# Weight matrices stored as contiguous blocks, and GpSimd's work around the routing softmax put behind it

## The chip, the cores and the metric

One core of one Trainium2 chip runs the whole program. The metric is the device time of one execution in microseconds (us). The median of 3 runs before is 2841.9 us, from 2841.22 to 2849.14. A profile of a further execution shows when each instruction ran on the five engines (PE, the matrix engine; DVE, VectorE; ACT, ScalarE; POOL, GpSimd; SP, which here only issues transfers) and what each transfer moved.

## The reference, cut to what matters

Two blocks run one after the other on 1024 tokens of 1024 features (float32).

The first block modulates a normalised input by vectors made from `silu(c) @ w_ada + b_ada`, multiplies it with `w_in` (1024 x 4624), runs a bidirectional recurrent memory (mLSTM) and a Fourier branch, merges the branches with `w_fourier` and `w_mlstm`, multiplies with `w_out`, and adds the result to `x`. It ends in a layer of 16 experts, each of which takes its 128 best tokens:

```python
def expert_choice(h, w_router, w_gate, w_up, w_down):
    b, l, _ = h.shape
    cap = CAP_FACTOR * l // N_EXPERTS
    aff = jax.nn.softmax(jnp.einsum('bld,de->ble', h, w_router).astype(jnp.float32), axis=-1)
    vals, idx = lax.top_k(jnp.swapaxes(aff, 1, 2), cap)
    bidx = jnp.arange(b)[:, None, None]
    xs = h[bidx, idx]
    hid = jax.nn.silu(jnp.einsum('becd,edf->becf', xs, w_gate)) * jnp.einsum('becd,edf->becf', xs, w_up)
    y = jnp.einsum('becf,efd->becd', hid, w_down) * vals[..., None].astype(h.dtype)
    return jnp.zeros_like(h).at[bidx, idx].add(y)
```

The second block has two layers of gated attention. Each computes `z = rms_norm(x) @ w_in`, cuts z into queries, keys, values and gates of several heads, attends, and returns `x + mixed @ w_out`. The even layer's `w_in` is 1024 x 4104, so a row of it is 16,416 bytes long; the odd layer's is 1024 x 3328, with rows of 13,312 bytes.

## The kernel before

**Products.** Every float32 product of a weight and an activation is made as three matmuls (`mm3`, lines 190 to 194) from a rounded high part and a low part of both operands. `split` (line 196) makes the parts: ACT or POOL copies the high part, and DVE or POOL subtracts it from the raw value for the low part.

**Weights.** Outside the experts, weights come in chunks of 256 columns. `Chunk.dma(j)` (line 1414) loads 128 columns of all 1024 rows into the tile `lwr` (128 partitions x 8 x 128, 512 KB), where row k*128+p of the matrix goes to partition p. The matrices lie in memory as the reference has them, row after row, so that such a load is 1024 pieces of 512 bytes, one row pitch apart. `Chunk.split(j)` makes `lwh` and `lwl` from it, on ACT and DVE. There are two `lwr` buffers. `w_ada` is loaded in blocks of 256 columns (tiles `wt` in `start`, line 327, and `awt` in `ada_late`, line 940), in pieces of 1024 bytes. A chunk of the merge takes three loads, from `w_fourier`, `w_fourier_r` and `w_mlstm` (line 223). The experts' weights (`ewr`, lines 977 to 991) are loaded in whole rows, pieces of 4096 bytes, through a ring of 13 buffers of 1 MB.

**Queues.** All these loads are issued by SP, in program order, and SP waits at a load until its buffer is free. ACT issues the small moves `qh<-qh` and `kY<-klo` of 128 KB, which carry the low or high part of queries and keys to the other half of the partitions (lines 1532 and 1548). POOL issues the experts' gathers and scatters.

**Attention.** `second` goes through units of four or fewer heads. `run_units` gives each slot the 24 matmuls of one token tile (`pz`, from `lwh`, `lwl` and the input's parts `lh`, `ll`) and, between them, steps of attention items that became ready earlier. `events` sets in which slot a chunk's load and split, a normalisation (`zq`, line 1511), and the making of queries and keys stand: the two `kY` moves are issued one slot after `keys`, and the items that read them (`psc<-kY,qh`, line 1872) start in that slot at the earliest.

**From the first block's output product to the experts.** `wout` runs over four column chunks and eight token tiles. In the last chunk each tile t gives `xg` (DVE, line 894), its transposes and the router's logits (PE, lines 899 and 902); after every second tile DVE computes 1/rms by a short chain on 128 x 2 numbers (`r4t`, `r4y`, lines 177 to 187, into `rst`), ACT scales the two `xg` tiles, POOL adds the shift `ada[:, 1]` (line 913), and SP writes them to `h2_d`. Then come the softmax over experts on `lt` (lines 919 to 926, with the Exp on ACT) and, in `experts`, `top_k`: PE transposes `lt` (line 1017), DVE finds 128 values of 64 rows with 16 rounds of MAX8, FIND_INDEX8 and MATCH_REPLACE8 (lines 1022 to 1026), and POOL gathers the chosen rows of `h2_d` into `xe` (line 1100), which the first expert's matmuls need. The first six low parts of the experts' weights are made by POOL (`ewl`, line 1066 with `n < 3`), the rest by DVE.

**What sets the order.** A compile-time scheduler orders each engine's instructions by readiness and by their place in the source; on the chip each engine runs its list strictly in order and waits at an instruction whose inputs or buffers aren't there.

Of the kernel before, what the change touches and what calls it, by code (L numbers as in the profile page):

```python
# [37 lines left out]
for _n, _w in (("bada", 16), ("g1", 8), ("conv", 72), ("wG", 8 * 16), ("bgi", 1), ("bgf", 1),  # L38
               ("rmask", 128), ("lmask", 128)):
    _pack(_n, _w, 1)  # L40


def host_arrays(i):
# [43 lines left out]
    for q in range(4):  # L87
# [14 lines left out]
        "pack0": packs[0], "pack1": packs[1], "x": g["x"][0], "ctx": g["ctx"][0], "w_ada": g["w_ada"][0], "b_ada": g["b_ada"][0],  # L102
        "w_in": wi, "dft_f": feat.astype(f), "dft_0": dc.astype(f), "dft_t": G[:, :512].astype(f),
        "dft_x": G[:, 512:].astype(f).reshape(8, 128, 2).transpose(1, 0, 2), "dft_n": odd.astype(f)[None],
        "w_fourier": wf[:, 1:65].reshape(256, D), "w_fourier_r": wf[:, 127:63:-1].reshape(256, D), "w_fourier_0": wf[:, 0], "w_mlstm": g["w_mlstm"][0], "w_out": g["w_out"][0],
# [46 lines left out]
class Kern:  # L152
# [54 lines left out]
    def first(self):  # L207
# [10 lines left out]
        cols = lambda off, i: Chunk(self, [w_in[:, off + i * 256 + j * 128:off + i * 256 + j * 128 + 128] for j in range(2)])  # L218
        pair = lambda w, c, j: w[:, c * 256 + j * 128:c * 256 + j * 128 + 128]
        qk, v, o, f = ([cols(off, i) for i in range(n)] for off, n in ((OFF_QK, 4), (OFF_V, 2), (OFF_O, 2), (OFF_F, 2)))  # L220
        br = [cols(OFF_BR, i) for i in range(8)]
        dg = [Chunk(self, [pair(a["dft_t"], c, j) for j in range(2)], *((a["dft_x"], 2) if c else ())) for c in range(2)]
        mg = [MergeChunk(self, [[pair(a[w], c, j) for w in ("w_fourier", "w_fourier_r", "w_mlstm")] for j in range(2)]) for c in range(4)]
        wo = [Chunk(self, [pair(a["w_out"], c, j) for j in range(2)]) for c in range(4)]
# [83 lines left out]
    def start(self, P, hp, cp, xr):  # L308
# [7 lines left out]
        wav = a["w_ada"].rearrange("(k p) n -> p k n", p=128)  # L316
# [8 lines left out]
        def load_w(b):  # L325
            wts[b] = P.tile([128, 8, 256], F32, name="wt", bufs=4)
            nc.sync.dma_start(out=wts[b], in_=wav[:, :, b * 256:(b + 1) * 256])
# [520 lines left out]
    def wout(self, P, mh, ml):  # L848
# [77 lines left out]
        nc.vector.tensor_tensor(lt, lt, bc(mx), op=OP.mult)  # L926
        nc.gpsimd.tensor_copy(self.ga2, ada[:, 3])

    def ada_late(self, P):
# [4 lines left out]
        wv = a["w_ada"].rearrange("(k p) n -> p k n", p=128)  # L934
# [111 lines left out]
    def experts(self, s):  # L1046
# [357 lines left out]
class Chunk:  # L1404
# [185 lines left out]
class OutProj:  # L1590


    def __init__(self, K, mx, w, x, out, gain, first=None):
        self.K, self.mx, self.x, self.out, self.gain, self.first = K, mx, x, out, gain, first
        self.chunks = [Chunk(K, [w[:, c * 256 + j * 128:c * 256 + j * 128 + 128] for j in range(2)]) for c in range(4)]
# [79 lines left out]
class UnitA(Unit):  # L1675
    def __init__(self, K, w, offs, u, h):
        super().__init__()
        self.K, self.u, self.h, self.kind = K, u, h, "a"
        self.chunks = [Chunk(K, [w[:, o:o + 128] for o in offs[2 * c:2 * c + 2]], *((K.a["wBF"], 8) if h == 0 and c == 0 else ())) for c in range(2)]
# [35 lines left out]
class UnitB(Unit):  # L1715
    def __init__(self, K, w, offs, u, kind, h0):
        Unit.__init__(self)
        self.K, self.u, self.kind, self.h0 = K, u, kind, h0
        self.chunks = [Chunk(K, [w[:, o:o + 128] for o in offs[2 * c:2 * c + 2]]) for c in range(2)]
# [293 lines left out]
```

## Time and profile before

| what | us |
|---|---|
| median of 3 runs (2841.22 to 2849.14) | 2841.9 |
| the profiled execution, its own time | 2847.84 |
| its span, first to last instruction | 2846.1 |
| PE busy in the span | 2674.4 |
| DVE busy | 2007.8 |
| ACT busy | 1351.0 |
| POOL busy | 398.1 |

The span lies 1.7 us under the execution's own time, and that execution 5.9 us above the median. A term worked out from the trace is one of the 2846.1 us. Busy time of PE is the sum over modelled matmul ends, so that a stretch with PE busy throughout can hold matmuls at half clock: the granted clock (PEclk, 1.00 is the full 2.4 GHz, 0.50 is 1.2 GHz) has to be read beside it.

### The profile page before, as it was taken

How to read it: one execution, taken by the hardware profiler on the slowest of the kernel's cores; microseconds unless marked ns; L12 is line 12 of the kernel's file. 1: busy time of each engine (PE TensorE's matmuls, PEld its weight loads, DVE VectorE, ACT ScalarE, POOL GpSimd, SP SyncE). 2: the span in 40 equal slices, each digit the busy share in tenths (PEclk: the TensorE clock that was granted, in tenths of full speed). 3: DMA queues.
4: the chain of work that ended last, by engine and by line, in shares of the span. 5: the costliest groups of instructions: out<-in, count | busy, mean ns of one | idle time of the engine just before them, and what ended most of it. 6: DMA issues, size and time to landing. Idle time of an engine off the chain costs nothing.

```text
span 2846.1 us, 48689 instructions
## 1 busy us (share of the span) xinstructions
PE 2674.4 (94%) x18222; PEld 2436.2 (86%) x18222; DVE 2007.8 (71%) x4915; ACT 1351.0 (47%) x2587; POOL 398.1 (14%) x487
## 2 busy tenths in 40 slices
PE   6999999999974999999987989999999999999999
PEld 4999887778963888888767989899999999999989
DVE  6677775566468999999967767766664677766652
ACT  5422322232233888877755544444453356544440
POOL 1000111015040111111121112111110011100000
PEclk9999999999976999999988999999999999999999
DMA  7222957665647999999945232323333422322133
GB/s 247 73 86 89 248 160 227 197 200 167 206 157 278 366 395 395 395 395 382 340 121 64 49 51 51 51 53 56 66 84 116 145 60 76 83 62 58 50 112 101
DMA packets 365902, 463.42 MB, mean 163 GB/s; under 512 B 19474, under 2 KB 279730, under 8 KB 365667
## 3 DMA queue, kind: packets, MB, share of 16 engines
q1 hardware_dynamic: 349410, 427.68, 47.1%
q0 software_dynamic: 7296, 17.96, 2.6%
q10 hardware_dynamic: 8960, 14.69, 2.2%
q8 instruction: 143, 2.34, 0.4%
q14 instruction: 93, 0.75, 0.1%
HBM read 387.80 MB, written 55.67 MB: 156 GB/s over the span
## 4 chain that ended last, share of the span: by engine, by line
PE 72%; DVE 11%; DMA 8%; issue 4%; ACT 3%; POOL 1%; SPq 0%; ACTq 0%; DVEq 0%; POOLq 0%
PE pz L192 7%; PE pz L194 7%; PE pz L193 7%; PE po L1942 4%; PE pT L192 3%; PE pT L193 3%; PE pT L194 3%; PE ptp L1928 2%; DMA kY<-klo 2%; PE pge L192 2%; PE pge L193 2%; PE pge L194 2%; PE pue L193 2%; PE pue L194 2%; PE pue L192 2%
## 5 line engine op out<-in xcount | busy, mean ns | idle before, releaser
L192 PE MATMUL pz<-lwh,lh 128*128 128x256 f32 (+1 forms) x2368 | 682.7, 288 | 8.9 <-ACT lh L199 6.3
L194 PE MATMUL pz<-lwh,ll 128*128 128x256 f32 (+1 forms) x2368 | 671.7, 284 | 3.3 <-DVE ll L204 2.0
L193 PE MATMUL pz<-lwl,lh 128*128 128x256 f32 (+1 forms) x2368 | 674.4, 285 | 0.0
L192 PEld LDWEIGHTS pz<-lwh,lh 128*128 128x128 f32 x2368 | 452.3, 191 | 13.2 <-ACT lh L199 7.4
L194 PEld LDWEIGHTS pz<-lwh,ll 128*128 128x128 f32 x2368 | 451.9, 191 | 5.3 <-DVE ll L204 3.3
L193 PEld LDWEIGHTS pz<-lwl,lh 128*128 128x128 f32 x2368 | 453.1, 191 | 1.9
L204 DVE TENSOR_TENSOR ewl<-ewr,ewh 128x1024 fp32r<-128x1024 f32 x372 | 435.5, 1221 | 11.9 <-ACT ewh L199 5.4
L199 ACT ACTIVATE ewh<-ewr 128x1024 fp32r<-128x1024 f32 x378 | 390.1, 1061 | 70.9 <-PE pue L194 24.9
L1911 ACT ACTIVATE S<-S,mx 128x128 f32<-128x128 f32 (+2 forms) x192 | 125.8, 655 | 179.2 <-DVE mx L1886 144.3
L1875 DVE CUSTOM_DVE_ANT_0 S<-psc,bias 128x512 f32<-128x512 f32 (+3 forms) x336 | 162.0, 497 | 34.0 <-PE psc L1873 33.1
L204 DVE TENSOR_TENSOR lwl<-lwr,lwh 128x1024 fp32r<-128x1024 f32 x128 | 158.3, 1242 | 34.3 <-ACT lwh L199 33.3
L199 ACT ACTIVATE lwh<-lwr 128x1024 fp32r<-128x1024 f32 x130 | 135.6, 1054 | 96.0 <-PE pT L193 35.2
L1942 PE MATMUL po<-vg,PT 128*128 128x64 f32 (+1 forms) x1344 | 173.1, 270 | 2.4 <-DVE PT L1933 1.9
L1942 PEld LDWEIGHTS po<-vg,PT 128*128 128x128 f32 x1344 | 165.0, 191 | 6.0 <-DVE PT L1933 3.1
L1492 POOL TENSOR_TENSOR hsq<-zq 128x256 f32<-128x256 f32 (+1 forms) x136 | 85.4, 628 | 563.7 <-ACT zq L1485 262.5
L1872 PE MATMUL psc<-kY,qh 128*128 128x512 f32 (+3 forms) x352 | 131.1, 376 | 35.2 <-DMA kY<-klo 24.6
L192 PE MATMUL pT<-hh,lwh 128*128 128x512 f32 x384 | 156.6, 408 | 3.0 <-ACT su L455 3.0
L193 PE MATMUL pT<-hl,lwh 128*128 128x512 f32 x384 | 153.9, 401 | 0.0
L194 PE MATMUL pT<-hh,lwl 128*128 128x512 f32 x384 | 153.2, 399 | 0.0
L1928 PE MATMUL ptp<-pack,S 128*128 128x128 f32 x792 | 132.6, 276 | 4.7 <-DVE PT L1933 2.0
L1133 POOL DMA_INDIRECT xacc<-ye,idx x32 | 67.4, 2108 | 438.0 <-DVE ye L1128 426.0
L1949 DVE SCALAR_TENSOR_TENSOR vg<-po,l,vg 128x64 f32<-128x64 f32 x192 | 54.2, 282 | 83.7 <-PE po L1942 82.1
(577 smaller groups left out, 6297.2 us busy)
## 6 DMA issues: line engine op xcount, KB each, us to landing
ewr<-in_w_gate_e SPq DMA_DIRECT2D x63, 1024.0 KB, 11.4
ewr<-in_w_up_e SPq DMA_DIRECT2D x63, 1024.0 KB, 8.1
ewr<-in_w_down_e SPq DMA_DIRECT2D x63, 1024.0 KB, 9.9
lwr<-in_w_in SPq DMA_DIRECT2D x36, 512.0 KB, 5.0
awt<-in_w_ada SPq DMA_DIRECT2D x32, 512.0 KB, 4.7
lwr<-in_even_w_in SPq DMA_DIRECT2D x32, 512.0 KB
lwr<-in_odd_w_in SPq DMA_DIRECT2D x26, 512.0 KB, 3.9
wt<-in_w_ada SPq DMA_DIRECT2D x8, 1024.0 KB, 11.3
```

The lines of the kernel that those rows point to most:

```text
L192: nc.tensor.matmul(out, ah, bh, start=start, stop=False)
L193: nc.tensor.matmul(out, ah, bl, start=False, stop=False)
L194: nc.tensor.matmul(out, al, bh, start=False, stop=stop)
L199: nc.scalar.activation(hi, raw, AF.Copy)
L204: (nc.vector if lo_eng == "dve" else nc.gpsimd).tensor_tensor(lo, raw, hi.bitcast(F32), op=OP.subtract)
L1133: nc.gpsimd.indirect_dma_start(out=self.xacc[c][:, :], out_offset=bass.IndirectOffsetOnAxis(ap=idx[:, e:e + 1], axis=0), in_=y[:, c * 512: ...
L1492: nc.gpsimd.tensor_tensor(sq[:, :n * 64], z, z, op=OP.mult)
L1872: nc.tensor.matmul(ps[:, :n], qh, k[:, ks], start=True, stop=False)
L1875: nc.vector.tensor_tensor_reduce(S[:, lo:hi], ps[:, lo - c0:hi - c0], bias, scale, -3e38, OP.add, OP.max, accum_out=mx[:, n_mx:n_mx + 1])
L1911: nc.scalar.activation(S[:, :nk], S[:, :nk], AF.Exp, bias=m, accum_out=l[:, 0:1])
L1928: nc.tensor.transpose(pt[:, i * 128:(i + 1) * 128], S[:, c0 + i * 128:c0 + (i + 1) * 128], K.ident)
L1942: nc.tensor.matmul(po[:, :dv], self.PT[i // 4][:, (i % 4) * 128:(i % 4 + 1) * 128], v(self.k0 // 128 + i), start=i == 0, stop=i == m - 1)
```

## The change

It does two things. First, the arrays are laid out anew before the kernel is called: `blocks` cuts a matrix into column blocks of 128 (of 256 for `w_ada`) and stores each block so that what one partition receives is contiguous. One load of `lwr` then is 128 pieces of 4096 bytes that follow each other in memory, and the same number of bytes. The three sources of a merge chunk become one matrix and one load. The 16 gate columns of `w_in` and the last 8 of the even layer's are left out of the blocks; they were loaded apart already. The experts' weights, and every activation that passes through memory, are as before.

```diff
+def blocks(w, n=128):
+    return np.asarray(w).reshape(-1, 128, w.shape[1] // n, n).transpose(2, 1, 0, 3)
...
-        "w_in": wi, ...
+        "w_in": blocks(np.concatenate([wi[:, :OFF_G], wi[:, OFF_BR:]], 1)), ...
-        "even_w_in": g["even_w_in_2"][0], "even_w_out": g["even_w_out_2"][0],
-        "odd_w_in": g["odd_w_in_2"][0], "odd_w_out": g["odd_w_out_2"][0],
+        "even_w_in": blocks(g["even_w_in_2"][0][:, :4096]), "even_w_out": blocks(g["even_w_out_2"][0]),
+        "odd_w_in": blocks(g["odd_w_in_2"][0]), "odd_w_out": blocks(g["odd_w_out_2"][0]),
...
-                nc.sync.dma_start(out=wt, in_=wv[:, 4 * kk:4 * kk + 4, c0:c0 + 256])
+                nc.sync.dma_start(out=wt, in_=a["w_ada"][8 + b][:, 4 * kk:4 * kk + 4])
...
-        parts = self.srcs[j] if isinstance(self.srcs[j], list) else [self.srcs[j]]
-        at = 0
-        for p in parts:
-            n = p.shape[0] // 128
-            K.nc.sync.dma_start(out=self.raw[j][:, at:at + n], in_=p.rearrange("(k p) n -> p k n", p=128))
-            at += n
+        K.nc.sync.dma_start(out=self.raw[j], in_=self.srcs[j])
```

Second, in `wout` the scaling, shifting and writing of the last two token tiles become a helper that is called after the softmax; the softmax's last multiplication goes from DVE to POOL; and these last tiles' additions, the copy of `ada[:, 3]` and the six `ewl` on POOL are bound to stand behind that multiplication in POOL's list.

```diff
+        def finish(t):
+            for i in range(2):
+                xg = xgs.pop(t - 1 + i)
+                nc.scalar.activation(xg, xg, AF.Copy, scale=rst[:, (t - 1 + i) % 4, t // 4:t // 4 + 1])
+                nc.gpsimd.tensor_tensor(xg, xg, ada[:, 1], op=OP.add)
+                nc.sync.dma_start(out=self.h2_d[(t - 1 + i) * 128:(t + i) * 128, :], in_=xg)
...
-            for i in range(2):
-                xg = xgs.pop(t - 1 + i)
-                nc.scalar.activation(xg, xg, AF.Copy, scale=rs[:, i:i + 1])
-                nc.gpsimd.tensor_tensor(xg, xg, ada[:, 1], op=OP.add)
-                nc.sync.dma_start(out=self.h2_d[(t - 1 + i) * 128:(t + i) * 128, :], in_=xg)
+            if t < 7:
+                finish(t)
...
-        nc.vector.tensor_tensor(lt, lt, bc(mx), op=OP.mult)
-        nc.gpsimd.tensor_copy(self.ga2, ada[:, 3])
+        self.softmax = nc.gpsimd.tensor_tensor(lt, lt, bc(mx), op=OP.mult).ins
+        with self.tc.issue_after(self.softmax):
+            finish(7)
+            nc.gpsimd.tensor_copy(self.ga2, ada[:, 3])
...
-                self.split(self.raws[n][k], wh, wl, lo_eng="pool" if n < 3 else "dve")
+                with ExitStack() as s:
+                    if n < 3:
+                        s.enter_context(self.tc.issue_after(self.softmax))
+                    self.split(self.raws[n][k], wh, wl, lo_eng="pool" if n < 3 else "dve")
```

On PE and ACT the same instructions stand in the same order as before, and on DVE one is gone, the last multiplication of the softmax (line 926). POOL's list before, from the last additions of `wout` (`xg`) over the low parts of the first weights (`ewl`) to the first gathers:

```order
L913 TENSOR_TENSOR xg_7877<-xg_7877,ada 128x1024
L913 TENSOR_TENSOR xg_7930<-xg_7930,ada 128x1024
L204 TENSOR_TENSOR ewl<-ewr,ewh 128x1024 x4
L913 TENSOR_TENSOR xg_8006<-xg_8006,ada 128x1024
L913 TENSOR_TENSOR xg_8059<-xg_8059,ada 128x1024
L204 TENSOR_TENSOR ewl<-ewr,ewh 128x1024 x2
L1100 DMA xe<-h_d,idx 128x1024 x4
```

The same place of POOL's list now (line numbers are those of the changed file):

```order
L878 TENSOR_TENSOR xg_7861<-xg_7861,ada 128x1024
L878 TENSOR_TENSOR xg_7914<-xg_7914,ada 128x1024
L935 TENSOR_TENSOR lt<-lt,mx_8084 128x8x16
L878 TENSOR_TENSOR xg_7990<-xg_7990,ada 128x1024
L878 TENSOR_TENSOR xg_8043<-xg_8043,ada 128x1024
L938 COPY ga_6713<-ada 128x1024
L210 TENSOR_TENSOR ewl<-ewr,ewh 128x1024 x6
L1113 DMA xe<-h_d,idx 128x1024 x4
```

The softmax's multiplication (`lt<-lt,mx`) has come in, and all six `ewl` and the copy now stand behind it. SP's list before, from the last write of the residual (`xacc`) over the writes of `h2_d` to the loads of the experts' weights:

```order
L883 DMA xacc_74<-xr_7873 128x256
L990 DMA ewr<-in_w_up_e 128x2x1024 x2
L914 DMA h_d<-xg_8006 128x1024
L914 DMA h_d<-xg_8059 128x1024
L1007 DMA ews<-in_w_up_e 128x1024 x2
L990 DMA ewr<-in_w_up_e 128x2x1024 x2
L990 DMA ewr<-in_w_gate_e 128x2x1024 x3
```

And now:

```order
L895 DMA xacc_74<-xr_7857 128x256
L879 DMA h_d<-xg_7990 128x1024
L879 DMA h_d<-xg_8043 128x1024
L1017 DMA ews<-in_w_up_e 128x1024 x2
L1000 DMA ewr<-in_w_up_e 128x2x1024 x2
L1000 DMA ewr<-in_w_gate_e 128x2x1024 x3
```

The two loads of `in_w_up_e` that stood ahead of the `h2_d` writes, and waited there for POOL's `ewl` to free their buffers, have moved behind the other loads of this stretch.

## Rows read from the trace of the kernel before

**Rows 1.** Stages: us, busy time by engine (instructions), granted clock, DMA share, GB/s.
```profile
450.00:625.00 175.00, 170.49 (x781) 136.12 (x780) 104.63 (x193) 43.46 (x78) 12.34 (x11) 0.97 0.65 199
...
1510.00:2120.00 610.00, 570.96 (x4582) 555.70 (x4583) 420.38 (x1550) 291.46 (x687) 110.10 (x186) 0.97 0.32 55
```
**Rows 2.** Waits of PE: line, releaser, us in total, times, longest.
```profile
PE pi L1035 <- DVE both L1031: 37.0, 1, 37.0
PE psc L1872 <- DMA kY<-klo: 24.6, 11, 8.7
...
PE pa L1017 <- DVE lt L926: 7.0, 1, 7.0
```
**Rows 3.** PE's timeline, even and odd layer: start, us, in brackets idle before, releaser.
```profile
1535.54 0.47 PE L1872 MATMUL psc<-kY,qh 128*128 128x128 f32 x1 [8.69 <-DMA kY<-klo]
...
2695.35 0.30 PE L1872 MATMUL psc<-kY,qh 128*128 128x128 f32 x1 [0.86 <-DMA kY<-klo]
```
**Rows 4.** Chain of waits: start, us from issue to landing of a kY move.
```profile
1677.21 13.33 DMA kY<-klo
...
2690.63 4.58 DMA kY<-klo
```
**Rows 5.** Windows in which weight loads run: even layer, odd layer, experts; columns as Rows 1.
```profile
1676.00:1680.00 4.00, 3.56 (x31) 3.56 (x32) 3.22 (x9) 1.20 (x3) 0.00 (x0) 1.00 0.77 66
...
2575.00:2579.00 4.00, 4.00 (x36) 3.92 (x35) 2.92 (x10) 1.38 (x5) 0.61 (x1) 1.00 0.84 241
...
1000.00:1100.00 100.00, 100.00 (x467) 83.35 (x466) 98.13 (x91) 82.12 (x85) 17.00 (x9) 1.00 1.03 394
```
**Rows 6.** Windows at low clock in the even layer; columns as Rows 1.
```profile
1529.50:1539.70 10.20, 4.16 (x17) 4.16 (x18) 2.77 (x17) 2.50 (x9) 0.46 (x1) 0.50 0.36 33
1686.50:1696.70 10.20, 6.11 (x28) 6.11 (x29) 4.11 (x25) 2.02 (x7) 1.50 (x2) 0.50 0.18 23
1843.50:1846.90 3.40, 3.40 (x18) 3.40 (x18) 1.88 (x12) 0.92 (x3) 0.46 (x1) 0.50 0.87 43
```
**Rows 7.** POOL's timeline around the softmax over experts: start, us.
```profile
831.69 10.34 POOL L204 TENSOR_TENSOR ewl<-ewr,ewh 128x1024 fp32r<-128x1024 f32 x4 [0.38 <-ACT ewh L199]
845.12 4.70 POOL L913 TENSOR_TENSOR xg<-xg,ada 128x1024 f32<-128x1024 f32 x2 [3.09 <-ACT xg L912]
849.78 4.65 POOL L204 TENSOR_TENSOR ewl<-ewr,ewh 128x1024 fp32r<-128x1024 f32 x2
```
**Rows 8.** DVE's timeline in the same stretch.
```profile
832.36 1.72 DVE L907 TENSOR_SCALAR v<-v 128x2 f32<-128x2 f32 x1
...
835.13 2.31 DVE L177 TENSOR_SCALAR r4t<-v 128x2 int32<-128x2 int32 x1
...
842.08 0.16 DVE L186 TENSOR_TENSOR r4t<-r4t,v 128x2 f32<-128x2 f32 x1
...
843.91 0.29 DVE L919 TENSOR_TENSOR lt<-logit,rst 128x128 f32<-128x128 f32 x1
...
846.87 0.74 DVE L926 TENSOR_TENSOR lt<-lt,mx 128x128 f32<-128x128 f32 x1
...
851.75 0.69 DVE L1023 MAX8 vals<-work 64x8 f32<-64x512 f32 x1
...
856.33 0.69 DVE L1023 MAX8 vals<-work 64x8 f32<-64x512 f32 x1
```
**Rows 9.** PE's timeline: the last router logits.
```profile
837.18 3.60 PE L902 MATMUL logit<-wR,h2T 128*128 128x16 f32 x16
```
**Rows 10.** ACT's timeline: the Exp of the softmax over experts.
```profile
845.99 0.29 ACT L923 ACTIVATE lt<-lt 128x128 f32<-128x128 f32 x1
```
**Rows 11.** POOL's instructions by shape: count, busy us, mean ns of one, idle before.
```profile
L1712 POOL TENSOR_TENSOR vg<-vg,sub 128x128 f32<-128x128 f32 x32 | 17.6, 549 | 115.9 <-DVE vg L1499 39.6 <-DVE hrt L186 23.5 <-DVE mx L1888 20.6
```
**Rows 12.** Transfers by line: count, KB each, median us to landing.
```profile
awt<-in_w_ada SPq DMA_DIRECT2D x32, 512.0 KB, 4.7
```
**Rows 13.** PE's timeline in the stage that loads awt.
```profile
464.89 0.79 PE L192 MATMUL pT<-hh,lwh 128*128 128x512 f32 x1 [2.98 <-ACT su L455]
```

More of the change, by code (lines that the diff above doesn't have):

```diff
@@ L101, in host_arrays @@
     d = {
-        "pack0": packs[0], "pack1": packs[1], "x": g["x"][0], "ctx": g["ctx"][0], "w_ada": g["w_ada"][0], "b_ada": g["b_ada"][0],
-        "w_in": wi, "dft_f": feat.astype(f), "dft_0": dc.astype(f), "dft_t": G[:, :512].astype(f),
+        "pack0": packs[0], "pack1": packs[1], "x": g["x"][0], "ctx": g["ctx"][0], "w_ada": blocks(g["w_ada"][0], 256), "b_ada": g["b_ada"][0],
+        "w_in": blocks(np.concatenate([wi[:, :OFF_G], wi[:, OFF_BR:]], 1)), "dft_f": feat.astype(f), "dft_0": dc.astype(f), "dft_t": blocks(G[:, :512].astype(f)),
         "dft_x": G[:, 512:].astype(f).reshape(8, 128, 2).transpose(1, 0, 2), "dft_n": odd.astype(f)[None],
-        "w_fourier": wf[:, 1:65].reshape(256, D), "w_fourier_r": wf[:, 127:63:-1].reshape(256, D), "w_fourier_0": wf[:, 0], "w_mlstm": g["w_mlstm"][0], "w_out": g["w_out"][0],
+        "w_merge": blocks(np.concatenate([wf[:, 1:65].reshape(256, D), wf[:, 127:63:-1].reshape(256, D), g["w_mlstm"][0]])),
+        "w_fourier_0": wf[:, 0], "w_out": blocks(g["w_out"][0]),
         "g_norm2": g["g_norm2"][0], "w_gate_e": g["w_gate_e"][0], "w_up_e": g["w_up_e"][0],
         "w_down_e": g["w_down_e"][0], "g_final": g["g_final"],
-        "even_w_in": g["even_w_in_2"][0], "even_w_out": g["even_w_out_2"][0],
-        "odd_w_in": g["odd_w_in_2"][0], "odd_w_out": g["odd_w_out_2"][0],
+        "even_w_in": blocks(g["even_w_in_2"][0][:, :4096]), "even_w_out": blocks(g["even_w_out_2"][0]),
+        "odd_w_in": blocks(g["odd_w_in_2"][0]), "odd_w_out": blocks(g["odd_w_out_2"][0]),
         "gln_o": g["odd_ln_g_2"][0],
@@ L217, in first @@
         w_in = a["w_in"]
[L218 to L224, printed above, removed]
+        pair = lambda w, i: [w[2 * i], w[2 * i + 1]]
+        qk, v, o, f, br = ([Chunk(self, pair(w_in, off // 256 + i)) for i in range(n)]
+                           for off, n in ((OFF_QK, 4), (OFF_V, 2), (OFF_O, 2), (OFF_F, 2), (OFF_G, 8)))
+        dg = [Chunk(self, pair(a["dft_t"], c), *((a["dft_x"], 2) if c else ())) for c in range(2)]
+        mg = [MergeChunk(self, pair(a["w_merge"], c)) for c in range(4)]
+        wo = [Chunk(self, pair(a["w_out"], c)) for c in range(4)]
         self.stream = [v[0], qk[2], v[1], qk[3], o[0], qk[0], o[1], qk[1], f[0], f[1], br[0], br[1], br[2], br[3], dg[0],
@@ L315, in start @@
         nc.vector.tensor_scalar(cs, cs, 0.5, None, op0=OP.mult)
-        wav = a["w_ada"].rearrange("(k p) n -> p k n", p=128)
         ss = P.tile([128, 12], F32, name="ss")
@@ L326, in load_w @@
             wts[b] = P.tile([128, 8, 256], F32, name="wt", bufs=4)
-            nc.sync.dma_start(out=wts[b], in_=wav[:, :, b * 256:(b + 1) * 256])
+            nc.sync.dma_start(out=wts[b], in_=a["w_ada"][b])
         self.hl, self.cl = Slabs([[None] * 2 for k in range(8)], 512), Slabs([[None] for k in range(8)], CTX)
@@ L933, in ada_late @@
         nc.vector.memset(ones, 1.0)
-        wv = a["w_ada"].rearrange("(k p) n -> p k n", p=128)
         for b in range(16):
@@ L1594, in __init__ @@
         self.K, self.mx, self.x, self.out, self.gain, self.first = K, mx, x, out, gain, first
-        self.chunks = [Chunk(K, [w[:, c * 256 + j * 128:c * 256 + j * 128 + 128] for j in range(2)]) for c in range(4)]
+        self.chunks = [Chunk(K, [w[2 * c], w[2 * c + 1]]) for c in range(4)]
         self.xt = {}
@@ L1678, in __init__ @@
         self.K, self.u, self.h, self.kind = K, u, h, "a"
-        self.chunks = [Chunk(K, [w[:, o:o + 128] for o in offs[2 * c:2 * c + 2]], *((K.a["wBF"], 8) if h == 0 and c == 0 else ())) for c in range(2)]
+        self.chunks = [Chunk(K, [w[o // 128] for o in offs[2 * c:2 * c + 2]], *((K.a["wBF"], 8) if h == 0 and c == 0 else ())) for c in range(2)]
         self.gains = lambda: [K.ga[:, h:h + 1], K.col("qkg")[:, 1:2]]
@@ L1718, in __init__ @@
         self.K, self.u, self.kind, self.h0 = K, u, kind, h0
-        self.chunks = [Chunk(K, [w[:, o:o + 128] for o in offs[2 * c:2 * c + 2]]) for c in range(2)]
+        self.chunks = [Chunk(K, [w[o // 128] for o in offs[2 * c:2 * c + 2]]) for c in range(2)]
         i = {"b": 2, "d": 6}[kind]
@@ L1761, in __init__ @@
         self.K = K
-        self.chunks = [Chunk(K, [w[:, 512:640], w[:, 640:768]])]
+        self.chunks = [Chunk(K, [w[4], w[5]])]
     def begin(self):
@@ L1802, in __init__ @@
         self.K, self.u, self.kv, self.h0, self.kind = K, u, kv, h0, "c"
-        self.chunks = [Chunk(K, [w[:, o:o + 128] for o in offs])]
+        self.chunks = [Chunk(K, [w[o // 128] for o in offs])]
     def begin(self):
```

## The prediction, made before the changed kernel ran

> **What bounds the kernel now.** I read the table of stages first. PE is busy for 2674.4 of the span's 2846.1 us, so all that the change can return is PE's 172 us of idle time, and what is lost where PE works at half clock. In the even layer (1510 to 2120 us) PE is idle for 610 - 571 = 39 us, at a granted clock of 0.97 [rows 1]. Then I read who PE waits for: 37.0 us for the end of the top-k, 24.6 us in 11 waits for the moves kY, and 7.0 us for the softmax's last multiplication [rows 2]. The change touches the last two of these directly.
>
> **The wait for kY.** A kY move carries 128 KB and is issued by ACT, yet one issued at 1677.21 us took 13.33 us to land; in the odd layer the same move, made by the same code, took 4.58 us [rows 4]. PE's longest wait for it is 8.69 us in the even layer, 0.86 us in the odd one [rows 3]. What differs are the weight loads that SP has just issued. While they run, the transfer engines are busy at a share of 0.77 and move 66 GB/s in the even layer, 0.84 and 241 GB/s in the odd one [rows 5]: 86 and 287 GB/s for a full share. Both load 512-byte pieces; only the row pitch differs, 16,416 against 13,312 bytes. A load of 512 KB thus takes 6.1 us of all engines in one layer and 1.8 us in the other, and a kY issued just behind two of them lands after them. Pieces of 4096 bytes that follow each other are what the experts' loads are, and these run at 394 GB/s [rows 5]; at that rate a block takes 1.3 us, and two take 2.7 us, where they now take 12.2 us. I take this rate for the new blocks, since their pieces are like those of the experts; the odd layer's 287 GB/s is the lower end.
>
> So a kY should land in 4 us or a little less, as in the odd layer. The move of 1677.21 us, for instance, then lands near 1681.3, where it landed at 1690.5. Of the 24.6 us I expect 21 to go: the odd layer shows that waits of under 1 us can stay [rows 3], and PE may run into DVE a little earlier. The ends are 0 (the loads are not the cause) and 24.6.
>
> After such a wait PE runs at half clock. In the three low stretches behind the kY waits PE was busy for 4.16, 6.11 and 3.40 us at 0.50 [rows 6]; half of these 13.7 us, 6.8 us, would not have been needed at full clock. With the waits gone I take 5 us of it; the ends are 0 and 6.8. DVE doesn't take this back at once: it was busy for only 2.77 of 10.2 and 4.11 of 10.2 us in the two longer stretches [rows 6].
>
> Two sentences of the Trainium skill bear on this and can be left out. "DMA: Bandwidth & Descriptors", Specifications, puts the size from which a transfer runs at line rate at 512 bytes; by that the 512-byte pieces gain nothing and the even layer's rate has another cause. [...]
>
> **The softmax and the top-k.** POOL ran four ewl from 831.69 us for 10.34 us [rows 7]. In that time DVE's short operations on 128 x 2 numbers, 0.16 us each when alone, took 1.72 us once and about 2.3 us three times (the row of 2.31 stands for the three) [rows 8]. That is 1.72 - 0.16 + 3 x (2.3 - 0.16) = 8 us more on the way to the softmax. With no ewl ahead of it DVE would be ready at 843.91 - 8 = 836 us, but the softmax then has to wait for the logits, which end at 837.18 + 3.60 = 840.8 us [rows 9]. These follow an xg of DVE that comes 1.6 us earlier too, so the logits end near 839.2, and the softmax's first operation goes from 843.91 to 839.3: 4.6 us. Before, Exp came at 845.99 us, 2.1 us after that operation [rows 10], though the four short operations of DVE between them need some 4 x 0.33 = 1.3 us (0.29 us each [rows 8], and the step to the next): ACT was still scaling xg. As 1/rms is ready earlier by more than the logits, these 0.8 us go too: 5.4 us. The multiplication itself took 0.74 us on DVE beside POOL [rows 8]. On POOL the nearest row is 0.55 us for 128 x 128 [rows 11], to which some 0.2 us for the way between the engines is added (the gap between instructions of two engines in this chain): no change.
>
> PE's 7.0 us and all behind it, the top-k and the first expert, thus come 5.4 us earlier. Lower end: 3 us (the logits come no earlier and the hand-over costs more); upper end 8 us (the whole excess).
>
> What now stands behind the multiplication on POOL: two xg, the copy and six ewl, 4.70 + 10.34 + 4.65 us and about 1.3 for the copy [rows 7], 21 us, from 842.5 to 864 us. Who waits for that: the writes of h2_d and the ewl, which the first gather and the first expert's matmuls need at 882 and 889 us, when the top-k, 37 us [rows 2], is over; 18 us remain. ACT's ewh are in the same order and have their six buffers. The loads that SP no longer holds ahead of the h2_d writes fill ring places 13 and 14; a place is 12 matmuls of the 467 that PE does in 100 us [rows 5], 2.6 us, so they are wanted some 35 us after the first expert's start. All of this I cost at 0. If the cover failed it would cost the part of the 21 us that sticks out.
>
> There is one more price: POOL now works beside the top-k. If it held MAX8 and its kin as it held the short chain, where 10.34 us of POOL cost 8 us of DVE, 21 us of POOL would cost up to 16 us. The trace has this case: MAX8 took 0.69 us at 851.75, while POOL ran two ewl until 854.43, and 0.69 us at 856.33, when POOL was idle [rows 7, 8]. I take 0. The Trainium skill ("SBUF — State Buffer", Who interferes with whom) says that a VectorE instruction with one SBUF input outside the two-port modes does not contend with GpSimd; by that rule the price is 0, and the trace agrees.
>
> **The other loads.** In the stage of 450 to 625 us PE is idle for 4.5 us, at a clock of 0.97 over 175 us, which is some 5 us of work lost [rows 1]; its longest wait is 2.98 us for ACT's su [rows 13], whose buffer is freed by a write that stands in SP's queue behind awt loads. These take 4.7 us to land [rows 12]. Moving 4096-byte pieces they need less; I take 2 us, between 0 and 6. The start, the merge (one load for three) and the output projections have little PE idle time next to a weight load: 1 us, between -1 and 4.
>
> **The sum.** 21 + 5 + 5.4 + 2 + 1 = 34 us. The profiled execution of 2847.84 us would become 2814. The median of the runs is 5.9 us lower, so the median after is 2841.9 - 34 = 2808 us. With all upper ends, 24.6 + 6.8 + 8 + 6 + 4 = 49 us: 2793. With half of the kY term and the lower ends elsewhere, 13 + 3 = 16 us: 2826.
>
> **The rivals.**
> *The loads are not what delays kY.* PE keeps its waits and only the softmax's part comes: 2841.9 - 5.4 = 2836 us. For it speaks that the low clock behind a late kY shows at three places only [rows 6], though all eight units of the even layer have their loads. Against it speaks the odd layer, with the same instructions and pieces, and rates that differ by 287/86. The skill's figure of 512 bytes, named above, would lead here.
> *The gain turns into waits for DVE.* In the even layer DVE is busy for 420 of 610 us [rows 1]; if the attention items that kY delayed now meet DVE's other work, half of the 26 us goes: 2841.9 - 21 = 2821 us. Against it: DVE idle beside PE in the stalls [rows 6].
> *Contiguous blocks load slowly.* If a block that lies in one piece of memory were drawn at the even layer's 86 GB/s, the stage that loads awt would become transfer-bound. The 32 awt loads are 16.8 MB [rows 12], 195 us at 86 GB/s; the stage's other 18 MB (199 GB/s x 175 us, less awt) take 59 us at the stage's 199/0.65 = 306 GB/s. That is 254 us for a stage of 175: 79 us longer, less 5.4, 2916 us, slower than before. It decides from a rate of 16.8 MB/(175 - 59) us = 145 GB/s downwards. Against it stands the rate of the experts' loads, 394 GB/s, each of which reads rows that follow each other [rows 5].
>
> **How the numbers follow.** The forecast has 0.80, the first rival 0.10, the second 0.06, the third 0.04. The predicted time is 2808 us; its own range is 2793 to 2826. That holds the second rival; widened a little for the spread of runs, up to 7 us within the three, it is 2790 to 2829 us, and leaves out the first rival and the third and a tail of the forecast. About 0.3% (8.5 us) is what a measurement of this kernel can tell from no change. The first rival's 6 us lie within it. Faster by more: 0.85; within: 0.11; slower: 0.04.
>
> **What would show it.** Right: weight loads at 250 GB/s or more for a full share in the even layer, kY landing in under 5 us, less than 4 us left of PE's 24.6, the low-clock stretches behind them gone; r4t at 0.2 us each, the softmax's multiplication on POOL about 5 us earlier than 846.87 against the last logits' start, MAX8 still at 0.69, POOL done before the first gather. Wrong: kY still late beside fast loads; MAX8 longer; PE idle at the first expert for ewl; the awt stage's transfer share up.

## The result, and the profile after

The changed kernel takes 2810.0 us (median of four runs, 2807.1 to 2814.3) against 2844.9 us of the kernel before: a ratio of 0.988 with a 95% interval of 0.986 to 0.990, some 35 us less. The forecast was 2808 us, between 2790 and 2829. The profiled execution took 2807.79 us with a span of 2806.0. It is 40 us shorter than the profiled one of before, since that lay 3 us above its median and this one 2 below; so the terms are sized below by runs against runs, and the traces tell where the time went. Lines of the code have moved: L1872 of before is L1880 now, L926 is L935, L1089 is L1102, L1023 is L1033.

First the waits of PE (line, releaser, us in total, times, longest), which answer [rows 2]:

```profile
PE pi L1045 <- DVE both L1041: 37.0, 1, 37.0
...
PE pt L1102 <- DMA xe<-h_d,idx: 7.9, 1, 7.9
...
PE pa L1027 <- POOL lt L935: 2.8, 1, 2.8
...
PE psc L1880 <- DMA kY<-klo: 1.0, 3, 0.4
```

The wait for kY went from 24.6 us in 11 waits to 1.0 us in 3, that for the softmax's last multiplication from 7.0 to 2.8. The top-k stayed at 37.0. The wait for the first gather, xe, is 7.9 us now; there something was given back. In the trace of before it stood at 6.3:

```profile
PE pt L1089 <- DMA xe<-h_d,idx: 6.3, 1, 6.3
```

The windows (us, busy time by engine with instructions, granted clock, DMA share, GB/s) answer [rows 1] and [rows 5]: the awt stage, the even layer at its new place, and two windows in which weight loads of the even layer run:

```profile
450.00:625.00 175.00, 169.27 (x789) 135.90 (x788) 104.71 (x192) 43.20 (x78) 13.35 (x11) 0.99 0.62 202
1500.50:2087.50 587.00, 564.75 (x4616) 550.01 (x4615) 423.59 (x1582) 293.19 (x693) 111.22 (x188) 1.00 0.20 57
...
1657.00:1660.00 3.00, 2.50 (x23) 2.29 (x22) 2.94 (x7) 1.66 (x3) 0.00 (x0) 1.00 0.75 226
1767.50:1771.50 4.00, 3.28 (x25) 2.90 (x22) 3.06 (x12) 1.38 (x4) 1.25 (x2) 1.00 0.74 245
```

In the even layer PE idles for 587 - 565 = 22 us instead of 39 and is busy for 565 us instead of 571, its granted clock is 1.00 instead of 0.97, and the transfer engines move slightly more per us at a share of 0.20 instead of 0.32. The loads run at 226/0.75 = 301 and 245/0.74 = 331 GB/s for a full share, where it was 86 [rows 5].

Then the timelines around the softmax (start, us), one row of DVE and four of POOL, which answer [rows 7] and [rows 8], and the group of all MAX8 (count, busy us, mean ns):

```profile
830.85 0.16 DVE L183 TENSOR_SCALAR r4t<-v 128x2 int32<-128x2 int32 x1
...
838.86 0.40 POOL L935 TENSOR_TENSOR lt<-lt,mx 128x128 f32<-128x128 f32 x1 [10.03 <-DVE mx L934]
839.22 4.65 POOL L878 TENSOR_TENSOR xg<-xg,ada 128x1024 f32<-128x1024 f32 x2
...
844.79 13.86 POOL L210 TENSOR_TENSOR ewl<-ewr,ewh 128x1024 fp32r<-128x1024 f32 x6
879.77 1.02 POOL L1113 DMA_INDIRECT xe<-h_d,idx  x1 [21.11 <-issue]
...
L1033 DVE MAX8 vals<-work 64x8 f32<-64x512 f32 x16 | 11.0, 686 | 2.8 <-ACT work L1028 2.3
```

The short operation that took 2.31 us beside POOL takes 0.16 us. The multiplication on POOL takes 0.40 us (forecast 0.55 and 0.2 for the way). POOL is done with xg, ga2 and the six ewl at 858.65 us and idle for 21.1 us before the first gather, and the mean MAX8 is 0.69 us with POOL beside its first part. So far the working holds.

Last, 8 us around the first gather, after and before:

```profile
876.00:884.00 8.00, 0.50 (x2) 0.32 (x2) 2.41 (x13) 0.00 (x0) 1.97 (x2) 0.50 1.03 409
...
885.00:893.00 8.00, 0.87 (x4) 0.71 (x5) 1.88 (x11) 0.00 (x0) 1.95 (x2) 0.50 0.36 105
```

The gather, issued at 879.77 us, now starts inside a stream of weight loads at 409 GB/s; before, issued at 888.20, it ran alone. That is where PE's 6.3 us became 7.9.

### The profile page after: what moved, and what is told of

Its sections match the earlier page's. It is cut to its first block, busy times and chain, and to the rows that moved or that the text cites. A ratio compares the mean times of both kernels' runs of the same rounds, so it can differ in the third digit from the quotient of the medians.

```text
span 2806.0 us, 48669 instructions
## 1 busy us (share of the span) xinstructions
PE 2657.2 (95%) x18222; PEld 2418.3 (86%) x18222; DVE 1997.9 (71%) x4914; ACT 1350.0 (48%) x2587; POOL 401.9 (14%) x488
## 4 chain that ended last, share of the span: by engine, by line
PE 74%; DVE 12%; DMA 5%; issue 5%; ACT 3%; POOL 2%; SPq 0%; ACTq 0%; DVEq 0%; POOLq 0%
PE pz L198 8%; PE pz L200 8%; PE pz L199 8%; PE po L1950 5%; PE pT L198 3%; PE pT L199 3%; PE pT L200 3%; PE ptp L1936 2%; PE pge L198 2%; PE pge L199 2%; PE pge L200 2%; PE pue L199 2%; PE pue L200 2%; PE pue L198 2%; PE pde L199 2%
## 5 line engine op out<-in xcount | busy, mean ns | idle before, releaser
L205 ACT ACTIVATE ewh<-ewr 128x1024 fp32r<-128x1024 f32 x378 | 390.2, 1061 | 71.2 <-PE pue L200 24.6
L1880 PE MATMUL psc<-kY,qh 128*128 128x512 f32 (+3 forms) x352 | 128.5, 369 | 11.8 <-DVE mx L1883 9.9
```

What stands on the lines that cost most here:

```text
L205: nc.scalar.activation(hi, raw, AF.Copy)
L1880: nc.tensor.matmul(ps[:, :n], qh, k[:, ks], start=True, stop=False)
```

## The experiments

The theory: loads of w_in of the even layer run at a third of the rate of others because of their row pitch of 16,416 bytes; kY queued behind them lands late, PE waits and then runs at half clock. Its rivals are the piece of 512 bytes as such, and another cause than these loads. Beside that: the part on POOL is worth 5 us, POOL's work behind the softmax is hidden, and the gather pays for loads that moved behind others.

### The even layer's blocks alone

```
-        "even_w_in": g["even_w_in_2"][0], ...
+        "even_w_in": blocks(g["even_w_in_2"][0][:, :4096]), ...
...
+def cut(w, o):
+    return w[o // 128] if len(w.shape) == 4 else w[:, o:o + 128]
...
-        self.chunks = [Chunk(K, [w[:, o:o + 128] for o in offs])]
+        self.chunks = [Chunk(K, [cut(w, o) for o in offs])]
```

> The kernel before with w_in of the even layer alone stored as column blocks (4096-byte pieces that follow each other); everything else as before. Theory: the late kY came from these loads, so PE's 24.6 us of kY waits and the half-clock stretches behind them go, and with them some 26 us: 2819 us against 2844.9 (2813 to 2825), even layer's stage about 28 us shorter, the loads at 250 GB/s or more for a full share. Rival, that kY is late for another reason: 2841 to 2846 us, kY waits still above 20 us.

Measured: 2820.1 us against 2845.0, ratio 0.991 (0.989 to 0.993). PE's waits for kY:

```profile
PE psc L1881 <- DMA kY<-klo: 2.5, 4, 1.1
```

From the even layer's first scores (psc) to the issue of the first load that reads its result, the kernel needs 22.8 us less than before. Of the change's 35 us these 32 loads bring 25 (21 to 31 by the interval). The rival that kY is late for another reason has fallen.

### Two other row pitches, still pieces of 512 bytes

One kernel lays 512 columns of zeros behind w_in of the even layer, the other 8; the loads are those of before.

```
-        "even_w_in": g["even_w_in_2"][0], ...
+        "even_w_in": np.pad(g["even_w_in_2"][0], ((0, 0), (0, 4616 - g["even_w_in_2"][0].shape[1]))), ...
```

> The kernel before with 512 columns of zeros behind w_in of the even layer: the same 512-byte pieces, the row pitch 18,464 bytes instead of 16,416; as before, every second row starts 32 bytes off a multiple of 64. Three theories of why these loads crawl. Pitch near 16 KiB: loads at 250 GB/s or more, 2819 us (2813 to 2826). Rows that start off a multiple of 64 bytes: still near 86 GB/s, kY waits above 20 us, 2845 us (2841 to 2849). Pieces of 512 bytes as such: also 2845 us.

> The kernel before with 8 columns of zeros behind w_in of the even layer: 512-byte pieces, row pitch 16,448 bytes, 64 above 16 KiB, and every row starts on a multiple of 64 bytes. Pitch near 16 KiB: still near 86 GB/s, 2845 us (2841 to 2849). Rows that start off a multiple of 64 bytes: 250 GB/s or more, kY waits under 4 us, 2819 us (2813 to 2826). Pieces of 512 bytes as such: 2845 us.

Measured: 2821.5 us (ratio 0.991, 0.990 to 0.993) and 2823.2 us (0.993, 0.991 to 0.994). Their waits for kY, the first line with 18,464 bytes, the second with 16,448:

```profile
PE psc L1872 <- DMA kY<-klo: 2.9, 4, 0.9
```

```profile
PE psc L1872 <- DMA kY<-klo: 2.2, 5, 1.1
```

Over the stretch that the blocks shortened by 22.8 us these two are 22.8 and 21.3 us shorter: eight columns of zeros bring nearly all that the blocks bring in this layer. The piece of 512 bytes is thus not the cause, and neither single condition that I had set up holds: 18,464 bytes is off a multiple of 64 and cured, 16,448 is next to 16 KiB and cured. Both of my theories of the pitch expected one of the two to stay slow.

### The pitch taken away from one layer and given to the other

```
-        "even_w_in": g["even_w_in_2"][0], ...
+        "even_w_in": g["even_w_in_2"][0][:, :4096], ...
-        "odd_w_in": g["odd_w_in_2"][0], ...
+        "odd_w_in": np.pad(g["odd_w_in_2"][0], ((0, 0), (0, 4104 - g["odd_w_in_2"][0].shape[1]))), ...
```

> The kernel before with two other row pitches: w_in of the even layer without its last 8 columns, 16,384 bytes; w_in of the odd layer with 776 columns of zeros behind it, 16,416 bytes instead of 13,312. Both still load 512-byte pieces. The two runs with 18,464 and 16,448 bytes were both cured, so neither the piece size, nor nearness to 16 KiB, nor the 32 bytes off a multiple of 64 is enough alone. If it is this one pitch that crawls, near 16 KiB and 32 bytes off together: the even layer is about 23 us shorter, as in the run with blocks, and the odd layer gets kY waits and is 8 to 21 us longer (26 loads instead of 32): 2828 to 2841 us. If it was the place or the content of that one matrix: the even layer 23 us shorter and the odd one unchanged, 2820 us. If an exact power of two is as bad as 16,416: the even layer as before and the odd one 8 to 21 us longer, 2853 to 2866 us.

Measured: 2872.2 us (two runs) against 2843.9, ratio 1.010 (1.007 to 1.013). Waits of PE for kY; a window with weight loads of the odd layer, and the stretch from the even layer's output projection to the odd layer's end:

```profile
PE psc L1872 <- DMA kY<-klo: 20.7, 4, 10.2
...
2346.00:2354.00 8.00, 7.96 (x69) 7.63 (x69) 7.21 (x46) 6.01 (x23) 1.42 (x2) 1.00 0.75 113
2103.50:2748.40 644.90, 594.48 (x4872) 581.22 (x4873) 398.42 (x1524) 289.05 (x794) 49.19 (x91) 0.97 0.37 78
```

The same stretch in the kernel with 16,448 bytes, where nothing of it is changed:

```profile
2091.90:2688.50 596.60, 582.63 (x4872) 569.64 (x4873) 398.10 (x1524) 288.56 (x794) 49.48 (x91) 1.00 0.30 84
```

The even layer, at 16,384 bytes, is cured (24.3 us shorter over the stretch used above). The odd layer has the illness now: loads at 113/0.75 = 151 GB/s for a full share instead of 287 [rows 5], a wait of 10.2 us for a kY, the clock at 0.97, 645 - 594 = 50 us of PE idle instead of 14, and 48 us more in all. So it is the pitch, and not the place or content of one matrix. An exact 16 KiB is harmless. The size was off, and the time lies above all three forecasts: I had scaled the even layer's loss by the number of loads, 8 to 21 us. Beside kY's 20.7 us PE waited 10.2 us in one place at the end of the even layer's output projection, where the rows of the sum that DVE adds are queued on SP behind the first of these loads.

### Loads alone, with 17 pitches

```
+PITCHES = (13312, 13344, 16352, 16384, 16400, 16416, 16432, 16448, 16480, 16512, 16544, 18464, 20512, 24608, 8224, 32800, 12320)
...
+            use(lambda t: nc.sync.dma_start(out=t, in_=a["p16416"][:, c * 128:c * 128 + 128].rearrange("(k p) n -> p k n", p=128)))
```

> Nothing of the kernel, only its loads, measured by themselves: one after the other, 512 KB into the same 128 x 1024 tile in 512-byte pieces, four each from matrices of 1024 rows with 17 row pitches from 8,224 to 32,800 bytes, ahead of them four loads of contiguous blocks, and at the end four with pitch 16,416 in which a partition takes eight rows that follow each other instead of rows 128 apart. A load at the odd layer's rate (287 GB/s for all engines) should land in about 4 us, one at the even layer's (86) in about 8. If it is this one pitch: 16,416 alone near 8 us, all others near 4. If 32 bytes above a multiple of 4 KiB is the condition (18,464 isn't one): 8,224, 12,320, 16,416, 20,512, 24,608 and 32,800 near 8, the others near 4. If near 16 KiB and 32 bytes off a multiple of 64: 16,352, 16,416, 16,480 and 16,544 near 8. If the pitch itself makes it, the last four are as slow; if it is how the pieces of one queue follow each other, they land in 4 us.

Measured in one execution, in SP's timeline: start, and the us over which four loads of one matrix, each waiting for the one before, were issued (the landing of the last is not in it). L36 are contiguous blocks; L38, L40, L42 have 13,312, 13,344 and 16,352 bytes; L44 to L54 have 16,384, 16,400, 16,416, 16,432, 16,448 and 16,480; L58 has 16,544 and L60 18,464; L72 is 16,416 again, with eight rows that follow each other for each partition. Under them the first 16,416 load as DVE saw it, with its wait in brackets.

```profile
0.73 14.80 SPq L36 DMA_DIRECT2D raw<-in_blk  x4
19.98 15.78 SPq L38 DMA_DIRECT2D raw<-in_p  x4
40.47 15.09 SPq L40 DMA_DIRECT2D raw<-in_p  x4
60.13 26.06 SPq L42 DMA_DIRECT2D raw<-in_p  x4
93.45 16.44 SPq L44 DMA_DIRECT2D raw<-in_p  x4
114.89 16.41 SPq L46 DMA_DIRECT2D raw<-in_p  x4
136.36 31.37 SPq L48 DMA_DIRECT2D raw<-in_p  x4
174.46 16.55 SPq L50 DMA_DIRECT2D raw<-in_p  x4
195.79 16.68 SPq L52 DMA_DIRECT2D raw<-in_p  x4
217.57 19.52 SPq L54 DMA_DIRECT2D raw<-in_p  x4
...
263.74 16.69 SPq L58 DMA_DIRECT2D raw<-in_p  x4
285.29 15.48 SPq L60 DMA_DIRECT2D raw<-in_p  x4
...
409.48 31.08 SPq L72 DMA_DIRECT2D raw<-in_p  x4
...
147.56 1.22 DVE L33 TENSOR_TENSOR o<-o,raw 128x1024 f32<-128x1024 f32 x1 [11.23 <-DMA raw<-in_p]
```

Two pitches stand out, 16,416 with 31.4 us and 16,352 with 26.1, one on each side of 16,384 and 32 bytes from it. 16,480, at 96 bytes, is a little slow (19.5 us); 16,544, at 160 bytes, is not, nor are 16,384 and the pitches 16, 48 and 64 bytes above it, nor any that is 32 bytes off a multiple of 64 elsewhere (13,344 and 18,464 among the rows; all matrices not shown took 15.5 to 16.4 us). The nearest of the four theories is the third, near 16 KiB and 32 bytes off together, over a narrower reach than I wrote. Which rows a partition takes made no difference at 16,416 (L72). For one load by itself the block's gain over a harmless pitch is small: DVE waits 3.6 us for a block and 3.9 for 13,312 bytes.

### The part on POOL alone

```
-        nc.vector.tensor_tensor(lt, lt, bc(mx), op=OP.mult)
-        nc.gpsimd.tensor_copy(self.ga2, ada[:, 3])
+        self.softmax = nc.gpsimd.tensor_tensor(lt, lt, bc(mx), op=OP.mult).ins
+        with self.tc.issue_after(self.softmax):
+            finish(7)
+            nc.gpsimd.tensor_copy(self.ga2, ada[:, 3])
```

and the six ewl under the same edge, as in the change; all weights by rows.

> The kernel before with the part on POOL alone: the softmax's multiplication on POOL, and the last two xg additions, the copy of ga2 and six ewl behind it; all weights as before. Theory: PE's wait for the softmax falls from 7.0 to near 2.8 us and the top-k stays at 37.0 us, as in the changed kernel: 4 to 5 us, 2840 us (2838 to 2842). The first gather lands in 6 us instead of 4.3 if the moved loads of the experts are what holds it, and then 1.6 us of the gain are given back: 2841 us. Rival, that the 8 us of slow short operations came from the weight loads and not from POOL: no change, 2845 us.

Measured: 2840.0 us, ratio 0.998 (0.997 to 1.000): 4.9 us less, between 0.3 and 9 by the interval. Waits of PE, and DVE's r4t:

```profile
PE pt L1099 <- DMA xe<-h_d,idx: 7.3, 1, 7.3
PE pa L1024 <- POOL lt L931: 2.8, 1, 2.8
...
832.13 0.16 DVE L177 TENSOR_SCALAR r4t<-v 128x2 int32<-128x2 int32 x1
```

PE's wait behind the softmax fell by 4.2 us as forecast, the short operations are at 0.16 us with the matrices outside the experts loaded as before, and the gather cost 1.0 us more. The slow short operations came from POOL's ewl.

### Both parts without the other blocks

> The kernel before with two parts of the change: w_in of the even layer as blocks, and the part on POOL; all other weights row by row as before. Apart they gave 24.9 and 4.9 us. If the two add up and the other blocks bring some 5 us: 2815 us (2812 to 2818). If the other blocks bring nothing, as the 3 us forecast for them lies within the spread: 2810 us (2807 to 2812), like the changed kernel.

Measured: 2810.6 us, ratio 0.988 (0.986 to 0.991): the changed kernel's time. All other blocks together (w_ada, w_in, the merge, the odd layer, the output projections) bring nothing that the runs can tell; with an interval 13 us wide, that leaves room for the few us forecast for them.

### The gather ahead of the two loads

```
-        self.nc.sync.dma_start(out=into, in_=self.weights(n))
+        if self.ring in (14, 15):
+            with self.tc.issue_after(self.gathered):
+                self.nc.gpsimd.dma_start(out=into, in_=self.weights(n))
+        else:
+            self.nc.sync.dma_start(out=into, in_=self.weights(n))
...
+                if e < 2:
+                    self.gathered = g.ins
```

> The changed kernel with the two loads of w_up_e for ring places 13 and 14 issued by POOL behind the first gathers, instead of by SP among the other loads ahead of them. Theory: the first gather takes 5.9 us instead of 4.3 to land because the backlog of weight loads (403 to 414 GB/s until about 883 us) ends just before it; 2 MB less of it ends 5 us earlier, the gather lands in 4.3 us and PE's wait for it falls from 7.9 to 6.3: 2808.4 us (2806 to 2811) against 2810.0. Rival, that the gather is longer for another reason: 2810 us and a wait of 7.9. If the moved loads come too late for the first expert: above 2812 us with PE idle for ewl or ewh 35 us after the first expert's start.

Measured: 2807.0 us (2804.9 to 2812.5), ratio 0.988 (0.986 to 0.990). The time can't tell it from the changed kernel, the trace can. PE's wait; the window around the gather; and POOL's order:

```profile
PE pt L1106 <- DMA xe<-h_d,idx: 6.3, 1, 6.3
...
876.00:884.00 8.00, 1.46 (x7) 1.31 (x8) 1.30 (x8) 0.00 (x0) 2.76 (x3) 0.50 0.44 137
...
878.61 1.02 POOL L1117 DMA_INDIRECT xe<-h_d,idx  x1 [21.10 <-issue]
...
880.89 0.79 POOL L1002 DMA_DIRECT2D ewr<-in_w_up_e  x1
```

With 2 MB taken out of the backlog (POOL now issues them, behind the first two gathers) the window moves 137 GB/s, the gather runs as good as alone, and PE's wait is back at 6.3 us. In four traces with the part on POOL and the two loads still ahead of the gather (the changed kernel twice, the part on POOL alone, that part with the even layer's blocks) it is 7.3 to 7.9. PE doesn't wait for the moved weights.

### More work on POOL

```
-            nc.gpsimd.tensor_copy(self.ga2, ada[:, 3])
+            for _ in range(33):
+                nc.gpsimd.tensor_copy(self.ga2, ada[:, 3])
```

> The changed kernel with the copy of ga2 on POOL done 33 times instead of once: 32 x 1.04 = 33 us more work behind the softmax's multiplication, with the same result. The forecast cost the work behind the multiplication at nothing because 21.1 us were left before the first gather. If that is the cover, 33 - 21 = 12 us stick out: the first gather is issued 12 us later and the run takes 2822 us (2818 to 2826). If POOL's work was no hindrance at all up to the gather: 2810 us. If POOL beside the top-k slows it, which the forecast denied: MAX8 above 0.69 us and the top-k above 37.0 us, 2830 us or more.

Measured: 2823.6 us in one execution, 13.6 above the changed kernel's median. POOL's last copies and its first gather; waits of PE; groups of DVE in the top-k; and one of the two copies in the changed kernel, where POOL was idle by then:

```profile
865.80 29.76 POOL L939 COPY ga<-ada 128x1024 f32<-128x1024 f32 x27
895.84 1.02 POOL L1114 DMA_INDIRECT xe<-h_d,idx  x1 [0.27 <-POOL ga L939]
...
PE pi L1046 <- DVE both L1042: 38.6, 1, 38.6
PE pt L1103 <- DMA xe<-h_d,idx: 20.1, 1, 20.1
...
L1034 DVE MAX8 vals<-work 64x8 f32<-64x512 f32 x16 | 11.0, 686 | 2.8 <-ACT work L1029 2.3
...
L1040 DVE COPY both<-vals 32x128 f32<-32x128 f32 x1 | 1.1, 1052 | 0.0
L1042 DVE COPY both<-vals 32x128 f32<-32x128 f32 x1 | 1.0, 966 | 0.0
```

```profile
876.78 0.20 DVE L1039 COPY both<-vals 32x128 f32<-32x128 f32 x1
```

The cover is as large as the trace said: 34.6 us more work on POOL, 21.1 of them hidden, 13.8 us later at the first expert. MAX8 keeps its 686 ns beside POOL throughout. But the top-k is 1.6 us longer all the same: its two plain copies take 1.05 and 0.97 us instead of some 0.2. They come last, when in the changed kernel POOL has been done for 18 us.

### The two places mended, beside the changed kernel once more

```
-            self.stream[0].split(j, "pool")
+            self.stream[0].split(j, ("pool", "dve")[j])
```

together with the moved loads of the run with the gather first.

> The changed kernel with the two places mended where it gave back time: the two loads of w_up_e behind the first gathers on POOL, and the second half of the first chunk's lwl on DVE (where it stands behind DVE's last ac) instead of on POOL, where with block loads it starts 1.5 us earlier and runs beside DVE's ac, whose nine operations took 7.85 us instead of 5.86. Theory: 1.6 us less at the first gather and 2 to 3 less at the start: 2806 us (2804 to 2808). Rival, that the start varies for another reason (in kernels without blocks it varied by 5 us as well): only the 1.6 us, 2808.4 us, and the nine operations at 5.86 us all the same.

> The changed kernel itself once more, beside the mended one on the same chip: 2810 us (2807 to 2814), first pV near 54 us, PE's wait for the first gather near 7.9 us if the backlog of loads makes it, nine operations ac in 7.85 us.

Measured: 2808.58 us (ratio 0.986, 0.985 to 0.988) for the mended kernel and 2808.64 us (0.987, 0.985 to 0.989) for the changed one: no difference. PE's wait for the first gather is 6.3 us in the one and 7.5 in the other, too little for the runs to tell. Rows of DVE and PE in the start, and the window until PE's first pV (the first large product), in the mended kernel:

```profile
37.91 5.86 DVE L389 SCALAR_TENSOR_TENSOR ac<-wt,cs,ac 128x256 f32<-128x256 f32 x9
...
43.52 1.87 PE L395 MATMUL pa<-wt,cs 128*2 128x256 f32 x4
...
38.00:54.70 16.70, 11.76 (x45) 4.71 (x43) 9.81 (x20) 4.05 (x7) 2.58 (x1) 0.80 0.76 302
```

The same in the changed kernel's second trace:

```profile
36.75 7.86 DVE L389 SCALAR_TENSOR_TENSOR ac<-wt,cs,ac 128x256 f32<-128x256 f32 x9
...
37.00:55.10 18.10, 13.05 (x43) 5.27 (x41) 10.49 (x19) 4.02 (x7) 4.76 (x2) 0.72 0.68 277
```

DVE's nine operations are back at 5.86 us, and the start isn't: the first pV comes at 54.7 us here and at 55.1 there. In its place stands PE at half clock, which does four matmuls in 1.87 us; in the trace of before the same four took 1.02. My theory of the start has fallen: the longer operations were real and not what set the end. In the five traces with all weights in blocks the first pV comes at 53.7 to 55.6 us, in six of the seven others at 50.3 to 52.9, in one (18,464 bytes, start unchanged) at 55.4, and there the granted clock was low as well. From 37 us to the first pV the granted clock was 0.72 to 0.81 in the five and 0.87 to 1.00 in the six. Why it is lower with blocks stays open.

## Why the prediction was right, point by point

**kY and the half clock behind it, 21 + 5 us.** Right in mechanism and, taken together, in size. By the runs the even layer's loads alone bring 24.9 us (21 to 31), the traces show 22.8 us of it in that layer, PE's waits of 24.6 us are down to 1.0, a kY lands in 4.2 us at most (10.0 before, by the same view), and the low stretches of [rows 6] are gone (clock 1.00). The split was off. By the windows above PE's idle time in the even layer fell by 17 us and its busy time by 6; over the stretch from the first psc to the first load of the result, which holds the same instructions in both kernels, by 15.6 and 7.5. So the waits gave less than 21 and the clock more than 5, and that the two errors cancel is luck. What the waits didn't give came back as other waits, above all for ACT, before and after:

```profile
PE ptp L1928 <- ACT so L1564: 1.9, 7, 0.5
...
PE ptp L1936 <- ACT so L1572: 4.7, 9, 1.2
```

The rate of 301 to 331 GB/s lies between the odd layer's 287, my lower end, and the experts' 394, which I took; the terms don't hang on which. What the prediction read from 86 against 287 GB/s, that the pitch and not the piece makes the difference, is shown by the two other pitches. What it left unsaid is that no block is needed: 8 columns of zeros cure it. By the Trainium skill ("DMA: Bandwidth & Descriptors", Specifications) 512 bytes is the least size for line rate. The runs come near that at the harmless pitches (287 GB/s for a full share in the odd layer against 301 to 331 for the blocks; by itself a first load of pieces took 3.7 to 4.4 us against 3.5 to 3.6 for a block); at 16,416 bytes the size is not enough. The power-of-two pitches that the same page of the Trainium skill reports (Latency and other measured facts) begin at 512 KiB; no run here has one, and at 16 KiB the power of two itself is harmless.

**Softmax, 5.4 us.** Right. By the runs 4.9 us (0.3 to 9). By the traces 4.2 us between the last logits and the use of lt, the same in every kernel with this part, and the logits themselves end some 2 us earlier; about 1.2 us is given back at the gather.

**The loads' cover, 0.** This step was mis-sized, by 1.0 to 1.6 us. I asked when the two moved loads are wanted (35 us after the first expert's start: right, PE doesn't wait for them) and not what they run beside. The backlog of weight loads ends at about 884 us in the trace of before and of after, since two loads that were done early now stand at its end. A gather issued 8 us earlier meets it. The run with the gather first takes this away.

**POOL beside the top-k, 0.** Right for this change, and the cover is the 21 us that the trace showed. MAX8, which I looked at, is not slowed by POOL even over the whole top-k. But the top-k has other operations: its two copies are slowed fivefold when POOL works beside them. The Trainium skill ("SBUF — State Buffer", Who interferes with whom) tells the two apart: an operation with one input contends with GpSimd only in a mode with two ports, and copies, casts and tensor_scalar are named as those that can enter one. The traces agree for MAX8 (0.69 us) and the plain copies (0.2 against 1.0); the cast and the tensor_scalar that stand between the copies and read integers kept their 0.21 us. I had quoted only its first half.

**awt, 2 us.** By the traces 3.1 us: the stretch from PE's last pg (the stage before) to its last pT lasts 198.0 us on average in the seven traces with rows (196.9 to 200.1) and 194.9 in the five with blocks (192.2 to 196.2). It came for the smaller part where I put it: the longest wait for su is 4.1 us, where it was 2.98 [rows 13], PE's idle time in the stretch is 0.8 us less on average, and the rest is busy time at a granted clock of 0.98 to 1.00 instead of 0.97 to 0.98. Why the clock is higher there no run shows.

**The start, the merge and the projections, 1 us.** By the means of the same traces the merge gives about 1 us (its two groups overlap: 79.9 to 86.6 us with rows, 80.2 to 82.2 with blocks), and the start costs 3, cause open: a loss of some 2 us, below my lower end of -1. With awt's 3.1 that leaves about 1 us for all other blocks, where I had 3; the run without them shows no difference.

**The rivals.** That the loads are not the cause has fallen with the even layer's blocks alone. That the gain turns into waits for DVE came in small part only: DVE is busy for 424 of 587 us in the even layer, and PE's waits for it there grew by 1.4 us, those for ACT by 3.9. That blocks load slowly is refuted by 301 to 331 GB/s.

**The range.** The sum with the lower ends is 13 + 3 + 0 - 1 = 15 us and not 16, 2827 us and not 2826; the widened range of 2790 to 2829 holds both. The traces are 40 us apart and the runs 35: the forecast of 34 is met by the runs.

## What to carry to other kernels

When a small transfer lands late, look at what its engines carry at that time, and divide GB/s by the busy share: a large matrix that moves far below the others has something wrong in its layout, and a few columns of padding tell at little cost whether it is the pitch. Where work is brought forward, look at what it now runs beside: a transfer that ran alone may come into a backlog whose end hasn't moved. And before a second engine is set beside a chain, look at every kind of operation in the chain, not at the one that takes most of it.

## What the runs showed of the hardware that I had not expected

A row pitch of 16,416 or 16,352 bytes, 32 bytes to either side of 16 KiB, makes loads in 512-byte pieces about one and a half to three times as long (a first load of 512 KB at 16,416 kept DVE waiting for 11.2 us, at 16,352 for 9.5, at 13,312 for 3.9), and at 16,416 the four loads of one matrix became faster one after the other: 11.2, 9.1, 7.0 and 5.9 us. 16,384 bytes itself, and 16, 48 or 64 bytes more, cost next to nothing (16.4 to 16.7 us for the four, 15.8 at 13,312). No run here shows why.

DVE's copies of 32 x 128 numbers took 0.97 to 1.05 us beside copies on POOL, about the length of one such copy (1.03 us where one stood alone), and 0.20 when POOL was idle, while MAX8 in the same stretch kept its 0.69 us to the hundredth.
